# A PSUM bank per head for the logits of a two-layer DSA and MLA decoder, 64-row products in pairs, and latent transposes ahead of the reads of their bank

## The chip, the cores and the metric

The kernel runs on one core of one Trainium2 chip. The metric is the time of one execution in device microseconds; smaller is better. The engines: TensorE (PE) does matrix products, with weight loads (PEld) beside them, VectorE (DVE) and ScalarE (ACT) elementwise work, GpSimd (POOL) a few small operations, and SyncE (SP) issues most DMAs. PE writes its products into PSUM, which has eight banks; a tile of 128 partitions by 512 fp32 fills one.

## What is computed

The reference runs two post-norm layers on 256 tokens of width 2048. In each, two groups of eight heads read the same x. Group A (DSA) keeps for each query the best keys by an indexer of 16 heads of 64; group B (MLA) has queries and keys of 128 columns without and 64 with rotation, from normalised latents. A SwiGLU FFN of 5632 follows.

```python
for i in range(DEPTH):
    mix = _hybrid_mixer(x, positions, w_in[i], g_cq[i], g_ckv[i], w_uq[i], w_ukv[i], w_o[i])
    x = _layer_norm(ALPHA * x + mix, ln1_g[i], ln1_b[i])
    ffn = _swiglu(x, w_gate[i], w_up[i], w_down[i])
    x = _layer_norm(ALPHA * x + ffn, ln2_g[i], ln2_b[i])
...
q_b = jnp.einsum('bsr,re->bse', _rms_norm(cq, g_cq), w_uq).reshape(b, s, MLA_HEADS, MLA_NOPE + MLA_ROPE)
q_nope, q_pe = q_b[..., :MLA_NOPE], _rope(q_b[..., MLA_NOPE:], positions, MLA_ROPE, MLA_ROPE_THETA)
q_mla = jnp.concatenate([q_nope, q_pe], axis=-1)
k_mla = jnp.concatenate([k_nope, k_pe], axis=-1)
out_b = _causal_attention(q_mla, k_mla, v_b, (MLA_NOPE + MLA_ROPE) ** -0.5)
```

## The kernel before, in words

Weights come in units of 256 rows by 512 columns and are split into two parts (`parts`): ACT rounds the high part `wh` (L308), DVE subtracts it for the low part `wl` (L309). Each product of a projection is then three (L330 to L332: high by high, low by high, high by low). The 256 tokens are two tiles t of 128. The projections follow one another; what belongs to attention is written as tasks (generators) that `tick()` takes a step further between weight units. Behind that, a scheduler orders the instructions anew on each engine, so that the order of the code is not that of the chip; engines wait for one another by semaphores on tiles.

PSUM is shared by turns: `acc()` gives banks 0 to 3 (projections), `trp()` 4 and 5 (transposes), `att()` 6 and 7 (attention).

An attend (`attend`, two heads j) takes one bank for each token tile t. MLA's `logits` (L646) writes a 128-row product of `qn` and `kn` (L652) and adds a 64-row one of `qpT` and `kpT` (L653), head by head and tile by tile: 128 columns for t = 0, 256 for t = 1. The rows of `qpT` lie by head pairs on one half of the partitions. DVE scales and masks (L455), the softmax follows, PE transposes the weights and multiplies with the values (the PV step, L474, L475) into a bank of `att()`. The products here are fp32, unsplit. There are four MLA attends and four DSA attends per layer. The indexer (L581) multiplies 64-row operands in pairs, on both halves of the partitions, into two banks.

`tb_post` normalises the latents (`rms`) and transposes them: for each tile t, `rms_T` of k into `ckvT` (PE L350, then ACT L353 for the high and DVE L354 for the low part), `dup_T` of the rotated key into the same bank and on to `kpT` (ACT L521), and `rms_T` of q into `cqT`.

In the FFN, 10 of 11 chunks of 512 columns run through `gate_up`, which computes gate and up (`c11`, `c21`, `c12`, `c22`: the part of token tile 0 or 1 in gate or up) with Winograd's seven products p1 to p7 in place of eight for half of the rows. p2, p4 and p3 are added into c11, c21 and c12 in PSUM; DVE combines the rest at the chunk's end: L894 (e), L899 (v), L900, L905 (g, from c21), L906, L907 (v, reads c22), L911 (e, reads c12). `hidden` then multiplies (L820), and PE transposes its result (T). Every second chunk has a group of the down projection inside (`group`). `BANKS` gives each product its bank: c11 4, c21 5, c12 6, c22 7, p1 0, p5 to p7 1 to 3.

Of the kernel before, what the change touches and what calls it, by code (L numbers as in the profile page):

```python
# [31 lines left out]
P = 128  # L32
# [46 lines left out]
def hybrid_trunk(ctx: ExitStack, tc: tile.TileContext, x, xt_in, pos, w_in, g_cq, g_ckv, w_uq,  # L79
# [46 lines left out]
    def in_turn(s, first, n):  # L126
        turns[s] = turns.get(s, -1) + 1
        return bank(first + turns[s] % n, s)
# [7 lines left out]
    def att():  # L136
        return in_turn("att", 6, 2)

# [306 lines left out]
    def attend(logits_of, scale, bias, v_of, oh, ol, h0):  # L445


        lgs = []
        for t in range(NT):
            n = P * (t + 1)  # L450
            lp = att()
            for j in range(2):
                logits_of(h0 + j, t, lp[:, j * n:(j + 1) * n], n)
            lg = t2([P, 2, n], "lg")
            nc.vector.scalar_tensor_tensor(  # L455
                lg, lp[:, :2 * n].rearrange("p (j n) -> p j n", j=2), scale,
                bias[t].unsqueeze(1).to_broadcast([P, 2, n]), op0=ALU.mult, op1=ALU.add)
            for j in range(2):
                softmax_head(lg[:, j, :], t, n)
            lgs.append(lg)  # L460
        yield 3
        prs = []
        for j in range(2):
            tp = trp()
            transpose4([lgs[0][:, j, :], lgs[1][:, j, 0:P], lgs[1][:, j, P:]], tp)
            pr = t2([P, 3 * P], "pr")
            nc.scalar.activation(pr, tp[:, :3 * P], AF.Copy)
            prs.append(pr)
        yield 1
        op = att()  # L470
        for j, pr in enumerate(prs):
            v0, v1 = v_of(h0 + j)
            ov = op[:, j * S:(j + 1) * S]
            mm(ov, v0, pr[:, 0:S], start=True, stop=False)  # L474
            mm(ov[:, P:], v1, pr[:, S:], start=False, stop=True)  # L475
        split(oh.rearrange("p j t -> p (j t)"), ol.rearrange("p j t -> p (j t)"), op)


    def layer(l, xh, xl, norms, last):
# [37 lines left out]

        def dup_T(dst, t, s, tp):

            transpose4([s.rearrange("p a b -> p (a b)")], tp)  # L520
            nc.scalar.activation(dst[:, t * P:(t + 1) * P], tp[:, :P], AF.Copy)  # L521

        def ta_post(o):
            ss = []
            for t in range(NT):
                nc.vector.tensor_scalar(wi[t], o[t][:, 0:I_HEADS], IW_SCALE, None, ALU.mult)
                ss.append(dup_rope(o[t][:, 16:80], cosI[t], sinI[t], I_ROT))
                nc.scalar.activation(cq[t][:, 0:432], o[t][:, 80:512], AF.Copy)
            yield 2
            for t in range(NT):  # L530
                dup_T(kiT, t, ss[t], trp())

# [10 lines left out]

        def rms_T(y, n, dst, t, tp):
            transpose4([y[:, i * P:(i + 1) * P] for i in range(n // P)], tp)
            tv = tp[:, :n].rearrange("p (k t) -> p k t", t=P)
            split(dst[:, 0, :, t * P:(t + 1) * P], dst[:, 1, :, t * P:(t + 1) * P], tv)

        def tb_post(o):
# [12 lines left out]
            for t, (yk, yq) in enumerate(ys):  # L562
                yield 1
                tp = trp()
                rms_T(yk, KVL, ckvT, t, tp[:, P:])
                dup_T(kpT, t, sd[t], tp)
                rms_T(yq, QL, cqT, t, trp())

        def indexer():
            yield from behind(p_ta, p_qi0, p_qi1)  # L570
            score = [pt([P, P * (t + 1)], F32, f"score{t}") for t in range(NT)]
            for t in range(NT):
                n = P * (t + 1)
                per = C // n
                for h0 in range(0, I_HEADS, 2 * per):
                    rp = [att() for _ in range(2)]
                    for j in range(per):
                        for r in range(2):
                            h = h0 + 2 * j + r
                            pr = slice(64 * r, 64 * r + 64)  # L580
                            mm(rp[r][:, j * n:(j + 1) * n], qiT[h // 8][pr, h // 2 % 4, t * P:(t + 1) * P],  # L581
                               kiT[pr, :n], start=True, stop=True)
                    rl = []
                    for r in range(2):
                        s = t2([P, per, n], "rel")
                        nc.scalar.activation(s.rearrange("p j n -> p (j n)"), rp[r], AF.Relu)
                        rl.append(s)
# [52 lines left out]
        def mla_attend(hp, m, wait, *before):  # L640
# [6 lines left out]

            def logits(h, t, dst, n):
                r = h // 2 % 2
                pr = slice(64 * r, 64 * r + 64)  # L650
                ts = slice(t * P, (t + 1) * P)
                mm(dst, qn[:, h % 4, ts], kn[:, h % 4, :n], start=True, stop=False)  # L652
                mm(dst, qpT[pr, 2 * (h // 4) + h % 2, ts], kpT[pr, :n], start=False, stop=True)  # L653

# [18 lines left out]
        def dsa_attend(hp, kaT, qaT, va, wait, *before):  # L673
# [5 lines left out]

            def logits(h, t, dst, n):  # L680
                mm(dst, qaT[:, h % 4, t * P:(t + 1) * P], kaT[:, h % 4, :n], start=True, stop=True)

# [147 lines left out]

        BANKS = {"c11": 4, "c21": 5, "c12": 6, "c22": 7, "p1": 0, "p5": 1, "p6": 2, "p7": 3}
        INTO = {"p2": "c11", "p4": "c21", "p3": "c12"}

        def gate_up(fc, plain, wino, between):
# [4 lines left out]
            def passes(name, lhs, ks, w, final):  # L839
                if name not in o:  # L840
                    o[name] = bank(BANKS[name], "gu_" + name)
                for j, k in enumerate(ks):
# [204 lines left out]
```

## Time and profile before

| | |
|---|---|
| median of 3 runs | 2238.47 us (2237.68 to 2239.29) |
| the profiled execution | 2240.56 us, of which the span is 2238.5 us |
| mean granted clock of TensorE | 0.996 of full speed |
| PE busy | 2194.0 us, 98% |
| DVE busy | 1702.2 us, 76% |
| ACT busy | 1193.1 us, 53% |

The profile is of one execution. PE is busy nearly throughout, so its own timeline and the list of what it waited for are the views to start with; the busy share of another engine says little until it is taken stretch by stretch.

### The profile page before, as it was taken

How to read it: one execution, taken by the hardware profiler on the slowest of the kernel's cores; microseconds unless marked ns; L12 is line 12 of the kernel's file. 1: busy time of each engine (PE TensorE's matmuls, PEld its weight loads, DVE VectorE, ACT ScalarE, POOL GpSimd, SP SyncE). 2: the span in 40 equal slices, each digit the busy share in tenths (PEclk: the TensorE clock that was granted, in tenths of full speed). 3: DMA queues.
4: the chain of work that ended last, by engine and by line, in shares of the span. 5: the costliest groups of instructions: out<-in, count | busy, mean ns of one | idle time of the engine just before them, and what ended most of it. 6: DMA issues, size and time to landing. Idle time of an engine off the chain costs nothing. (4 is left out here: it accounts for less than half of the span.)

```text
span 2238.5 us, 27874 instructions
## 1 busy us (share of the span) xinstructions
PE 2194.0 (98%) x10128; PEld 1809.4 (81%) x10128; DVE 1702.2 (76%) x2215; ACT 1193.1 (53%) x1537; POOL 110.2 (5%) x198
## 2 busy tenths in 40 slices
PE   8999999999999999999999999999999999999997
PEld 7878788788888887887777887887888888888885
DVE  6675556987968788699667756569879697887985
ACT  5555443654555555555545554445546555555563
POOL 0100000100000000100101000001000100000002
PEclk9999999999999999999999999999999999999998
DMA  8544445656576766756655455556655757576574
GB/s 300 162 154 149 143 166 181 242 170 207 180 234 206 245 189 225 201 204 201 204 173 166 141 166 165 174 174 226 206 186 201 223 201 244 178 250 210 193 258 115
DMA packets 126057, 437.04 MB, mean 195 GB/s; under 512 B 14320, under 2 KB 14368, under 8 KB 125664
## 3 DMA queue, kind: packets, MB, share of 16 engines
q1 hardware_dynamic: 113760, 409.26, 54.0%
q0 software_dynamic: 12160, 26.01, 5.9%
q8 instruction: 79, 1.29, 0.2%
q14 instruction: 58, 0.48, 0.1%
HBM read 416.33 MB, written 2.10 MB: 187 GB/s over the span
## 5 line engine op out<-in xcount | busy, mean ns | idle before, releaser
L309 DVE TENSOR_TENSOR wl<-raw,wh 128x1024 fp32r<-128x1024 f32 (+1 forms) x892 | 1068.9, 1218 | 448.8 <-ACT wh L308 441.9
L308 ACT ACTIVATE wh<-raw 128x1024 fp32r<-128x1024 f32 (+1 forms) x892 | 926.9, 1055 | 873.9 <-PE acc L332 392.1
L846 PE MATMUL gu_c<-wh,xh 128*128 128x512 f32 x800 | 314.1, 393 | 6.7 <-DVE g L905 6.5
L848 PE MATMUL gu_c<-wl,xh 128*128 128x512 f32 x800 | 311.3, 389 | 0.0
L849 PE MATMUL gu_c<-wh,xl 128*128 128x512 f32 x800 | 311.3, 390 | 0.0
L330 PE MATMUL acc<-wh,xh 128*128 128x512 f32 (+1 forms) x768 | 303.0, 395 | 6.3 <-ACT wh L308 6.3
L331 PE MATMUL acc<-wl,xh 128*128 128x512 f32 (+1 forms) x768 | 299.1, 389 | 3.6 <-DVE wl L309 3.6
L332 PE MATMUL acc<-wh,xl 128*128 128x512 f32 (+1 forms) x768 | 297.9, 388 | 0.0
L330 PE MATMUL acc<-wh,hT 128*128 128x512 f32 x640 | 249.0, 389 | 0.9 <-DVE v L906 0.9
L331 PE MATMUL acc<-wl,hT 128*128 128x512 f32 x640 | 249.1, 389 | 0.5 <-DVE wl L309 0.5
L332 PE MATMUL acc<-wh,hT 128*128 128x512 f32 x640 | 248.8, 389 | 0.0
L871 DVE TENSOR_TENSOR raw<-raw,raw 128x1024 f32<-128x1024 f32 x160 | 195.5, 1223 | 8.4 <-DMA raw<-in_w_up_dram 5.0
L846 PEld LDWEIGHTS gu_c<-wh,xh 128*128 128x128 f32 x800 | 150.2, 188 | 41.0 <-DVE g L905 10.2
L849 PEld LDWEIGHTS gu_c<-wh,xl 128*128 128x128 f32 x800 | 150.2, 188 | 31.5
L330 PEld LDWEIGHTS acc<-wh,xh 128*128 128x128 f32 x768 | 144.7, 189 | 37.9 <-ACT wh L308 7.1
L848 PEld LDWEIGHTS gu_c<-wl,xh 128*128 128x128 f32 x800 | 150.2, 188 | 30.5 <-DVE wl L309 0.3
L331 PEld LDWEIGHTS acc<-wl,xh 128*128 128x128 f32 x768 | 145.3, 189 | 32.0 <-DVE wl L309 6.1
L332 PEld LDWEIGHTS acc<-wh,xl 128*128 128x128 f32 x768 | 145.0, 189 | 27.9
L330 PEld LDWEIGHTS acc<-wh,hT 128*128 128x128 f32 x640 | 120.1, 188 | 26.2 <-DVE v L906 1.3
L331 PEld LDWEIGHTS acc<-wl,hT 128*128 128x128 f32 x640 | 120.1, 188 | 25.7 <-DVE wl L309 0.9
L332 PEld LDWEIGHTS acc<-wh,hT 128*128 128x128 f32 x640 | 120.1, 188 | 24.9
L941 POOL DMA_DIRECT2D x<-d x64 | 55.0, 875 | 1135.4 <-ACT d L940 1108.5
(235 smaller groups left out, 2611.3 us busy)
## 6 DMA issues: line engine op xcount, KB each, us to landing
raw<-in_w_gate_dram SPq DMA_DIRECT2D x176, 512.0 KB, 4.7
raw<-in_w_up_dram SPq DMA_DIRECT2D x176, 512.0 KB, 4.7
raw<-in_w_down_dram SPq DMA_DIRECT2D x176, 512.0 KB, 5.1
raw<-in_w_in_dram SPq DMA_DIRECT2D x144, 512.0 KB, 3.4
raw<-in_w_o_dram SPq DMA_DIRECT2D x64, 512.0 KB, 3.3
x<-d POOLq DMA_DIRECT2D x64, 256.0 KB, 6.4
raw<-in_w_in_dram SPq DMA_DIRECT2D x16, 400.0 KB, 3.0
raw<-in_w_uq_dram SPq DMA_DIRECT2D x12, 512.0 KB, 3.3
```

The lines of the kernel that those rows point to most:

```text
L308: nc.scalar.activation(wh[:, :n], raw[:, :n], AF.Copy)
L309: nc.vector.tensor_tensor(wl[:, :n], raw[:, :n], f(wh[:, :n]), op=ALU.subtract)
L330: mm(o[t][:, :n], h, a, start=first, stop=False)
L331: mm(o[t][:, :n], h, b, start=False, stop=False)
L332: mm(o[t][:, :n], l, a, start=False, stop=final)
L846: mm(o[name], h, a, start=name not in begun, stop=False)
L848: mm(o[name], h, b, start=False, stop=False)
L849: mm(o[name], l, a, start=False, stop=end)
L871: nc.vector.tensor_tensor(d, x, y, op=ADD)
L941: nc.gpsimd.dma_start(sl, d, accum_op=ALU.add)
```

## The change

`att()` gives one tile over both banks 6 and 7. An attend takes one such tile, with a bank for each head in place of one for each token tile: the four 128-row products of MLA go first, then the 64-row ones in pairs, head 0 on partitions 0 to 63, head 1 on 64 to 127 (the host's permutation of the columns goes). Both token tiles' masks read that tile. The PV result takes a bank of `trp()`. The indexer's two banks come as one tile too, and so do c12 and c22 of `gate_up`. In `tb_post` all three transposes of a token tile come ahead of the reads of their banks.

```diff
     def att():
-        return in_turn("att", 6, 2)
+        return ps.tile([P, 2, C], F32, name=nm("att"), tag="b67", bufs=1)
...
+        lp = att()
+        logits_of(h0, [[lp[:, j, 0:P], lp[:, j, P:3 * P]] for j in range(2)])
         for t in range(NT):
             n = P * (t + 1)
-            lp = att()
-            for j in range(2):
-                logits_of(h0 + j, t, lp[:, j * n:(j + 1) * n], n)
             lg = t2([P, 2, n], "lg")
...
-        op = att()
+        op = trp()
...
-                tp = trp()
-                rms_T(yk, KVL, ckvT, t, tp[:, P:])
-                dup_T(kpT, t, sd[t], tp)
-                rms_T(yq, QL, cqT, t, trp())
+                tp, tq = trp(), trp()
+                rms_T(yk, KVL, tp[:, P:])
+                dup_T(sd[t], tp)
+                rms_T(yq, QL, tq)
+                rms_out(KVL, ckvT, t, tp[:, P:])
+                dup_out(kpT, t, tp)
+                rms_out(QL, cqT, t, tq)
...
-            def logits(h, t, dst, n):
-                r = h // 2 % 2
-                pr = slice(64 * r, 64 * r + 64)
-                ts = slice(t * P, (t + 1) * P)
-                mm(dst, qn[:, h % 4, ts], kn[:, h % 4, :n], start=True, stop=False)
-                mm(dst, qpT[pr, 2 * (h // 4) + h % 2, ts], kpT[pr, :n], start=False, stop=True)
+            def logits(h0, dst):
+                ts = [slice(t * P, (t + 1) * P) for t in range(NT)]
+                for j in range(2):
+                    for t in range(NT):
+                        h = (h0 + j) % 4
+                        mm(dst[j][t], qn[:, h, ts[t]], kn[:, h, :P * (t + 1)], start=t == 0, stop=False)
+                for t in range(NT):
+                    for j in range(2):
+                        pr = slice(64 * j, 64 * j + 64)
+                        mm(dst[j][t], qpT[pr, h0 // 2, ts[t]], kpT[pr, :P * (t + 1)], start=False, stop=t == NT - 1)
...
-        BANKS = {"c11": 4, "c21": 5, "c12": 6, "c22": 7, "p1": 0, "p5": 1, "p6": 2, "p7": 3}
+        BANKS = {"c11": 4, "c21": 5, "p1": 0, "p5": 1, "p6": 2, "p7": 3}
...
                 if name not in o:
-                    o[name] = bank(BANKS[name], "gu_" + name)
+                    if name in BANKS:
+                        o[name] = bank(BANKS[name], "gu_" + name)
+                    else:
+                        pair = att()
+                        o["c12"], o["c22"] = pair[:, 0, :], pair[:, 1, :]
```

What this does to the order of the instructions is seen at three places. First, PE at the latents of layer 0: `dup` is the rotated key, `rn` a normalised latent, `qiT` the indexer's queries, `acc` a projection. Before, from the dup transpose of tile 0 to the transposes of tile 1:

```order
L330 MATMUL acc_1039<-wh_1156,xh_67 128x512
L350 MATMUL tr_1140<-ident,dup_981 128x128 [waits DVE_49]
L331 MATMUL acc_1039<-wl_1157,xh_67 128x512
L332 MATMUL acc_1039<-wh_1156,xl_69 128x512
L581 MATMUL att_1172<-kiT_393,qiT_82 128x256 [waits Activation_49]
L581 MATMUL att_1173<-kiT_393,qiT_82 128x256 [waits Activation_49]
L581 MATMUL att_1172<-kiT_393,qiT_82 128x256
L581 MATMUL att_1173<-kiT_393,qiT_82 128x256
L350 MATMUL tr_1186<-ident,rn_1019 128x128 [waits Activation_49]
L350 MATMUL tr_1186<-ident,rn_1019 128x128
L350 MATMUL tr_1193<-ident,rn_1027 128x128 [waits DVE_49]
L350 MATMUL tr_1193<-ident,rn_1027 128x128 x3
```

After, the transposes of tile 0, and then what stands ahead of those of tile 1:

```order
L333 MATMUL acc_1036<-wh_1119,xl_69 128x512
L351 MATMUL tr_1135<-ident,rn_1000 128x128 [waits DVE_49]
L351 MATMUL tr_1135<-ident,rn_1000 128x128
L351 MATMUL tr_1135<-ident,dup_978 128x128
L351 MATMUL tr_1136<-ident,rn_1008 128x128 [waits DVE_49]
L351 MATMUL tr_1136<-ident,rn_1008 128x128 x3
```

```order
L332 MATMUL acc_1036<-wl_1152,xh_67 128x512
L333 MATMUL acc_1036<-wh_1151,xl_69 128x512
L589 MATMUL att_1167<-kiT_393,qiT_82 128x256 [waits PE_49,Activation_49]
L589 MATMUL att_1167<-kiT_393,qiT_82 128x256 x3
L351 MATMUL tr_1180<-ident,rn_1016 128x128 [waits Activation_49]
L351 MATMUL tr_1180<-ident,rn_1016 128x128
L351 MATMUL tr_1180<-ident,dup_990 128x128
L351 MATMUL tr_1181<-ident,rn_1024 128x128 [waits DVE_49]
```

The dup transpose of tile 0 has moved from the middle of a projection unit, where it waited for DVE, to the other transposes of its tile; those of tile 1 wait for ACT, which copies to kpT.

Second, PE at the end of an FFN chunk of layer 0 (`gu_c21`, `gu_c12`, `gu_c11` and the tile `att` are c21, c12, c11, and c12 with c22, with running numbers behind; p3 is the product with `s`). Before, p3 stands behind c21's last products (p4), and the next chunk's c11 follows:

```order
L846 MATMUL gu_c211080_5067<-wh1145_5372,xh779_3632 128x512
L848 MATMUL gu_c211080_5067<-wl1146_5373,xh779_3632 128x512
L849 MATMUL gu_c211080_5067<-wh1145_5372,xl780_3633 128x512
L846 MATMUL gu_c121087_5098<-wh1148_5386,s4827_3861 128x512 [waits Activation_49]
L848 MATMUL gu_c121087_5098<-wl1149_5387,s4827_3861 128x512 [waits DVE_49]
L849 MATMUL gu_c121087_5098<-wh1148_5386,s4828_3862 128x512
L846 MATMUL gu_c121087_5098<-wh1148_5386,s4827_3861 128x512
L848 MATMUL gu_c121087_5098<-wl1149_5387,s4827_3861 128x512
L849 MATMUL gu_c121087_5098<-wh1148_5386,s4828_3862 128x512
L846 MATMUL gu_c111156_5410<-wh1154_5406,xh763_3513 128x512 [waits DVE_49,Activation_49]
L848 MATMUL gu_c111156_5410<-wl1155_5407,xh763_3513 128x512 [waits DVE_49]
```

After, p4 is followed by 24 products of the next chunk (c11, then c21), of which the last two are seen here, then p3:

```order
L870 MATMUL gu_c211140_5400<-wl1143_5410,xh765_3618 128x512
L871 MATMUL gu_c211140_5400<-wh1142_5409,xl766_3619 128x512
L868 MATMUL att1071_5082<-wh1131_5369,s4813_3847 128x512 [waits DVE_49]
L870 MATMUL att1071_5082<-wl1132_5370,s4813_3847 128x512
L871 MATMUL att1071_5082<-wh1131_5369,s4814_3848 128x512
L868 MATMUL att1071_5082<-wh1131_5369,s4813_3847 128x512
L870 MATMUL att1071_5082<-wl1132_5370,s4813_3847 128x512
L871 MATMUL att1071_5082<-wh1131_5369,s4814_3848 128x512
L351 MATMUL tr1149_5451<-ident_70,silu1135_5384 128x128 [waits DVE_49]
L351 MATMUL tr1149_5451<-ident_70,silu1135_5384 128x128 x3
L868 MATMUL att1147_5431<-wh1145_5427,xh749_3499 128x512 [waits DVE_49,Activation_49]
```

p3 has moved behind 24 products of the next chunk, and its first product waits for DVE alone.

Third, DVE at the same chunk end. Before, from L900 to the product with the up part:

```order
L900 TENSOR_TENSOR e1134_5320<-e1134_5320,gu_p51105_5178 128x512 [waits DVE_49]
L905 TENSOR_TENSOR g11147_5382<-gu_c211080_5067,v71144_5368 128x512 [waits PE_49]
L911 TENSOR_TENSOR e1134_5320<-e1134_5320,gu_c121087_5098 128x512 [waits DVE_49,PE_49]
L906 TENSOR_TENSOR v71144_5368<-v71144_5368,gu_p51105_5178 128x512 [waits DVE_49]
L820 TENSOR_TENSOR silu1151_5398<-silu1151_5398,e1134_5320 128x512 [waits DVE_49,Activation_49]
L907 TENSOR_TENSOR v71144_5368<-v71144_5368,gu_c221088_5105 128x512 [waits DVE_49]
L309 TENSOR_TENSOR wl1175_5499<-raw1173_5496,wh1174_5498 128x1024 [waits DMAHW0_49]
L820 TENSOR_TENSOR silu1152_5401<-silu1152_5401,v71144_5368 128x512 [waits DVE_49,Activation_49]
```

After, from L922 (L900 before), with g at L927 (L905), v at L928 and L929 (L906, L907), and e at L933 (L911):

```order
L922 TENSOR_TENSOR e1117_5303<-e1117_5303,gu_p51088_5161 128x512 [waits DVE_49]
L927 TENSOR_TENSOR g11130_5365<-gu_c211064_5051,v71127_5351 128x512 [waits PE_49]
L310 TENSOR_TENSOR wl1152_5461<-raw1150_5458,wh1151_5460 128x1024 [waits DMAHW7_49,Activation_49]
L928 TENSOR_TENSOR v71127_5351<-v71127_5351,gu_p51088_5161 128x512 [waits DVE_49]
L310 TENSOR_TENSOR wl1157_5481<-raw1155_5478,wh1156_5480 128x1024 [waits DMAHW0_49,Activation_49]
L929 TENSOR_TENSOR v71127_5351<-v71127_5351,att1071_5082 128x512 [waits DVE_49]
L310 TENSOR_TENSOR wl1160_5499<-raw1158_5496,wh1159_5498 128x1024 [waits DMAHW1_49,Activation_49]
L838 TENSOR_TENSOR silu1135_5384<-silu1135_5384,v71127_5351 128x512 [waits DVE_49,Activation_49]
L933 TENSOR_TENSOR e1117_5303<-e1117_5303,att1071_5082 128x512 [waits PE_49]
L310 TENSOR_TENSOR wl1163_5517<-raw1161_5514,wh1162_5516 128x1024 [waits DMAHW2_49,Activation_49]
L838 TENSOR_TENSOR silu1134_5381<-silu1134_5381,e1117_5303 128x512 [waits DVE_49]
```

Weight splits now stand between the additions, and the one that reads c12 has moved behind the one that reads c22 and the first product.

## Rows read from the trace of the kernel before

**Rows 1.** It is the page's part 1: busy time, share of the span and instructions of each engine, PE first.

```profile
PE 2194.0 (98%) x10128; PEld 1809.4 (81%) x10128; DVE 1702.2 (76%) x2215; ACT 1193.1 (53%) x1537; POOL 110.2 (5%) x198
```

**Rows 2.** The waits of PE in the whole span, grouped by what was waited for; columns: us in total, times, longest.

```profile
PE gu_c L846 <- DVE g L905: 6.5, 6, 1.7
PE tr L350 <- DVE ckvT L354: 6.4, 3, 3.1
PE acc L330 <- ACT wh L308: 6.3, 2, 5.9
```

**Rows 3.** PE's timeline over the first MLA attend, the start of the second and the last one; columns: start, duration, instruction, and in brackets idle time before it. An x2 row is the two passes of one fp32 product; the duration runs over both and past the next start.

```profile
151.12 0.39 PE L652 MATMUL att<-kn,qn 128*128 128x128 f32 x2
151.44 0.48 PE L653 MATMUL att<-kpT,qpT 64*128 64x128 f32 x2
...
152.68 0.70 PE L652 MATMUL att<-kn,qn 128*128 128x256 f32 x2
153.31 0.70 PE L653 MATMUL att<-kpT,qpT 64*128 64x256 f32 x2
...
155.19 0.50 PE L330 MATMUL acc<-wh,xh 128*128 128x512 f32 x1
155.53 0.39 PE L331 MATMUL acc<-wl,xh 128*128 128x512 f32 x1
...
164.13 0.39 PE L652 MATMUL att<-kn,qn 128*128 128x128 f32 x2
...
1372.74 0.39 PE L652 MATMUL att<-kn,qn 128*128 128x128 f32 x2
...
1376.82 0.50 PE L330 MATMUL acc<-wh,xh 128*128 128x512 f32 x1
```

**Rows 4.** PE's timeline over the start of the PV step of the first MLA attend (L474, L475: 256 and 128 columns, all with 128 contraction rows), same columns.

```profile
171.08 0.60 PE L474 MATMUL att<-pr,vb 128*128 128x256 f32 x2
171.51 0.38 PE L475 MATMUL att<-pr,vb 128*128 128x128 f32 x2
171.73 0.60 PE L474 MATMUL att<-pr,vb 128*128 128x256 f32 x2
```

**Rows 5.** PE's timeline over one step of the indexer (L581: four products of 64 rows and 256 columns, in pairs on the two halves of the rows and in two banks) and the projection's products behind it, same columns.

```profile
106.94 1.14 PE L581 MATMUL att<-kiT,qiT 64*128 64x256 f32 x8
108.00 0.50 PE L330 MATMUL acc<-wh,xh 128*128 128x512 f32 x1
108.34 0.40 PE L331 MATMUL acc<-wl,xh 128*128 128x512 f32 x1
```

**Rows 6.** Busy time of each engine in two stretches, with their number of instructions; the first is one FFN chunk from p7 to p7, the second the next chunk, which has a down group in it. Behind the engines: granted clock, DMA share, GB/s.

```profile
571.12:612.85 41.73, 41.73 (x189) 34.62 (x188) 40.26 (x42) 23.98 (x27) 0.00 (x0) 1.00 0.50 172
612.85:655.00 42.15, 41.70 (x188) 34.32 (x187) 28.94 (x30) 22.90 (x26) 3.50 (x4) 1.00 0.83 273
```

**Rows 7.** PE's timeline at the transposes of the latents, layer 0 and layer 1.

```profile
113.58 0.39 PE L330 MATMUL acc<-wh,xh 128*128 128x512 f32 x1
117.10 0.47 PE L350 MATMUL tr<-ident,dup 128*128 128x128 f32 x1 [3.13 <-DVE ckvT L354]
...
1228.42 0.33 PE L350 MATMUL tr<-ident,dup 128*128 128x128 f32 x1 [3.11 <-DVE ckvT L354]
```

**Rows 8.** The timeline of DVE and ScalarE (ACT) around the first of these.

```profile
115.49 1.22 DVE L309 TENSOR_TENSOR wl<-raw,wh 128x1024 fp32r<-128x1024 f32 x1
116.63 0.42 DVE L354 TENSOR_TENSOR ckvT<-tr,ckvT 128x256 fp32r<-128x256 f32 x1
...
117.61 0.28 ACT L521 ACTIVATE kpT<-tr 128x128 f32<-128x128 f32 x1 [4.73 <-PE tr L350]
```

**Rows 9.** Busy time and granted clock (the column behind POOL) in the stretches behind the two long latent waits, and in one of the FFN with a wait in it.

```profile
117.00:121.00 4.00, 3.90 (x18) 2.43 (x18) 1.87 (x3) 1.87 (x4) 0.00 (x0) 0.58 0.39 131
1228.50:1233.00 4.50, 4.50 (x20) 3.25 (x21) 2.93 (x6) 3.29 (x6) 0.00 (x0) 0.63 0.49 138
872.00:880.00 8.00, 6.30 (x29) 4.87 (x28) 7.24 (x11) 5.63 (x7) 0.00 (x0) 1.00 0.65 244
```

**Rows 10.** The timeline of PE and DVE at the end of a chunk at which DVE lags: p7's start, the subtraction g, and the first product that waits for it.

```profile
867.75 0.39 PE L846 MATMUL gu_p<-wh,s 128*128 128x512 f32 x1
...
874.56 0.68 DVE L905 TENSOR_TENSOR g<-gu_c,v 128x512 f32<-128x512 f32 x1
...
875.30 0.50 PE L846 MATMUL gu_c<-wh,xh 128*128 128x512 f32 x1 [1.70 <-DVE g L905]
```

**Rows 11.** The timeline of PE and DVE at the end of a chunk at which DVE runs on time: p7's start, and DVE's operations behind it.

```profile
571.13 0.39 PE L846 MATMUL gu_p<-wh,s 128*128 128x512 f32 x1
...
572.16 1.22 DVE L309 TENSOR_TENSOR wl<-raw,wh 128x1024 fp32r<-128x1024 f32 x1
...
573.29 0.68 DVE L899 TENSOR_TENSOR v<-e,gu_p 128x512 f32<-128x512 f32 x1
...
575.62 0.68 DVE L905 TENSOR_TENSOR g<-gu_c,v 128x512 f32<-128x512 f32 x1
...
576.22 0.68 DVE L911 TENSOR_TENSOR e<-e,gu_c 128x512 f32<-128x512 f32 x1
```

**Rows 12.** The timeline of DVE and PE behind the PV step of the first MLA attend: DVE's split of its result, and the next attend's transposes.

```profile
173.51 0.68 DVE L354 TENSOR_TENSOR oB<-att,oB 128x512 fp32r<-128x512 f32 x1
...
177.85 0.38 PE L350 MATMUL tr<-ident,lg 128*128 128x128 f32 x2
```

More of the change, by code (lines that the diff above doesn't have):

```diff
@@ L448, in attend @@
         lgs = []
+        lp = att()
+        logits_of(h0, [[lp[:, j, 0:P], lp[:, j, P:3 * P]] for j in range(2)])
         for t in range(NT):
             n = P * (t + 1)
-            lp = att()
-            for j in range(2):
-                logits_of(h0 + j, t, lp[:, j * n:(j + 1) * n], n)
             lg = t2([P, 2, n], "lg")
-            nc.vector.scalar_tensor_tensor(
-                lg, lp[:, :2 * n].rearrange("p (j n) -> p j n", j=2), scale,
-                bias[t].unsqueeze(1).to_broadcast([P, 2, n]), op0=ALU.mult, op1=ALU.add)
+            nc.vector.scalar_tensor_tensor(lg, lp[:, :, t * P:t * P + n], scale,
+                                           bias[t].unsqueeze(1).to_broadcast([P, 2, n]), op0=ALU.mult, op1=ALU.add)
             for j in range(2):
@@ L516, in dup_rope, with dup_T, dup_out @@
             return s
-        def dup_T(dst, t, s, tp):
+        def dup_T(s, tp):
             transpose4([s.rearrange("p a b -> p (a b)")], tp)
+        def dup_out(dst, t, tp):
             nc.scalar.activation(dst[:, t * P:(t + 1) * P], tp[:, :P], AF.Copy)
@@ L530, in ta_post @@
             for t in range(NT):
-                dup_T(kiT, t, ss[t], trp())
+                tp = trp()
+                dup_T(ss[t], tp)
+                dup_out(kiT, t, tp)
         def rms(src, n, g):
@@ L542, in rms, with rms_T, rms_out @@
             return y
-        def rms_T(y, n, dst, t, tp):
+        def rms_T(y, n, tp):
             transpose4([y[:, i * P:(i + 1) * P] for i in range(n // P)], tp)
+        def rms_out(n, dst, t, tp):
             tv = tp[:, :n].rearrange("p (k t) -> p k t", t=P)
@@ L575, in indexer @@
                 for h0 in range(0, I_HEADS, 2 * per):
-                    rp = [att() for _ in range(2)]
+                    rp = att()
                     for j in range(per):
@@ L580, in indexer @@
                             pr = slice(64 * r, 64 * r + 64)
-                            mm(rp[r][:, j * n:(j + 1) * n], qiT[h // 8][pr, h // 2 % 4, t * P:(t + 1) * P],
+                            mm(rp[:, r, j * n:(j + 1) * n], qiT[h // 8][pr, h // 2 % 4, t * P:(t + 1) * P],
                                kiT[pr, :n], start=True, stop=True)
@@ L585, in indexer @@
                         s = t2([P, per, n], "rel")
-                        nc.scalar.activation(s.rearrange("p j n -> p (j n)"), rp[r], AF.Relu)
+                        nc.scalar.activation(s.rearrange("p j n -> p (j n)"), rp[:, r, :], AF.Relu)
                         rl.append(s)
@@ L678, in dsa_attend, with logits @@
                 oT["A"] = [t8([P, A_HEADS, S], F32R, "oA") for _ in range(2)]
-            def logits(h, t, dst, n):
-                mm(dst, qaT[:, h % 4, t * P:(t + 1) * P], kaT[:, h % 4, :n], start=True, stop=True)
+            def logits(h0, dst):
+                for j in range(2):
+                    for t in range(NT):
+                        h = (h0 + j) % 4
+                        mm(dst[j][t], qaT[:, h, t * P:(t + 1) * P], kaT[:, h, :P * (t + 1)], start=t == 0,
+                           stop=t == NT - 1)
             h0 = 2 * hp
@@ L1027 @@
     q = np.arange(M_HEADS * (M_NOPE + M_ROPE)).reshape(M_HEADS, -1)
-    pe = q[[0, 2, 1, 3, 4, 6, 5, 7], M_NOPE:]
+    pe = q[:, M_NOPE:]
     args.append([given(f"w_uq{i}", _blocks(a["w_uq"], c.reshape(-1)))
```

## The prediction

> **What bounds the kernel now.** I read the page's busy times first. TensorE (PE) is busy 2194.0 of 2238.5 us [rows 1], so it is the bound almost everywhere, and this change takes no product away: time can come only from PE's few idle stretches, or from stretches in which it counts as busy and advances slowly. The waits of PE, grouped by what they wait for, come second [rows 2]: 6.5 us for a DVE subtraction at the ends of FFN chunks (L905), 6.4 us for a DVE subtraction on the latents (L354), and 6.3 us at the start, which the change leaves alone. For slow busy time I read PE's timeline around the MLA logits [rows 3], and compared it with the same products in other company [rows 4, 5]. VectorE (DVE) is second: over one chunk it is busy 40.26 of 41.73 us while PE is busy for all of it [rows 6], so there DVE's order decides when PSUM banks come free.
>
> **The logits: -14.9 us.** In an MLA attend eight products alternate between 128 contraction rows (L652) and 64 (L653). From the first product to the next projection's second one is 155.53 - 151.12 = 4.41 us, of which that projection's first product takes one spacing of 0.23: 4.18 us net [rows 3]. The last attend agrees: 1376.82 - 1372.74 = 4.08 against 155.19 - 151.12 = 4.07. The same widths without alternation cost 0.43 (256 columns) and 0.22 (128) in the PV step [rows 4]; I use 0.213 for the second, half of the first. Four of each make 2.57, so eight changes of shape cost 1.61, or 0.20 each. After the change there are two changes of shape, 0.40. The four 128-row products stay at 2 x (0.43 + 0.213) = 1.29. What two 64-row products on the two halves cost, the indexer shows: four of 256 columns into two banks take 108.34 - 106.94 - 0.23 = 1.17 us with both edges [rows 5], where one after another they would take 1.72 and the edges; so they overlap, and each pair costs about one of its products, 0.43 + 0.21 = 0.64. The sum is 1.29 + 0.64 + 0.40 = 2.33, a gain of 1.86 per attend, 14.9 for the eight. Bounds: with no overlap the pairs cost 1.29, and the gain is 6 x 0.20 = 1.2 each, 9.8 in all; if the edges cost nothing beyond 0.1 each, 16.6.
>
> **The latent transposes: -6.9 us.** Here the wait is PE's on the subtraction into ckvT: the transpose of dup writes the bank that this subtraction reads. PE has run out of work at 113.97 and stands until 117.10 (3.13 us) in layer 0, and 3.11 us at 1228.42 in layer 1; the third wait is 0.17 [rows 2, 7]. DVE was never idle meanwhile: the subtraction starts at 116.63, straight behind a weight split, and ends at 117.05 [rows 8]. After each long wait the granted clock is lower, 0.58 over 4 us and 0.63 over 4.5, between the levels 2.4 and 1.2 GHz [rows 9]: 4 x 0.42 + 4.5 x 0.37 = 3.35 us more. Together 6.4 + 3.35 = 9.75 us. The change puts dup's transpose ahead of the reads, so this wait goes, but a smaller one comes: the transposes of the second token tile take the same bank, which the copy to kpT, queued behind the same subtraction, must have read. Without the wait PE gets there after two products (0.45), the dup transpose (0.1) and an indexer step (1.2), at 113.81 + 1.75 = 115.6. The subtraction may come some 0.3 us earlier than now, ends near 116.75, and the copy takes 0.28 [rows 8]: 117.05. That leaves 1.45 us per layer, 2.9 in all. A stall of 1.70 us elsewhere left the clock at 1.00 [rows 9, 10], so I count no slow clock: 9.75 - 2.9 = 6.9. Bounds: 0.3 (the stall comes back at the second tile with the slow clock), and 9.75.
>
> **The FFN: +9.9 us.** What the change's words don't name is that c12 and c22 of gate_up now lie in one tile. The last product of a chunk, p3, writes c12; the DVE addition that reads c22 (L907) comes ahead of it in the program, and with one tile p3 waits for it, at all twenty chunk ends. The order of after bears it out: p3's six products no longer stand behind p4, but behind 24 products of the next chunk, and DVE's additions have weight splits between them (the third piece of order above). The DVE rows give the prices: a split or an addition of two raw tiles 1.135 from start to start, a 512-column addition 0.60 [rows 11]. From the start of g (L905) to the end of the c22 addition the new order takes 0.60 + 1.135 + 0.60 + 1.135 + 0.68 = 4.15 us. There are three waits, all of PE:
> (a) c21 of the next chunk, for g. It used to stand behind p3 and up to ten products; now 5.46 us (24 products at 0.2275) after p7's start. Where DVE runs on time, g ends 575.62 + 0.60 - 571.13 = 5.1 us after it: no wait [rows 11]. Where DVE lags, as at 867.75, g ends at 875.22, 7.47 after, and PE waits 2.0 us instead of 1.70 [rows 10]. Worked out so for the nine ends with a lag, the total is 10.5 us in place of 6.5: +4.0.
> (b) p3, for the c22 addition. After c21 come 12 products (2.73 us); the addition ends 4.15 - 0.60 = 3.55 after g. That is 0.8 where nothing else stands between, and at the ends with four or five filler products nothing: five ends of layer 0 together, +2.8.
> (c) The next c12, for the addition that reads p3's result (L911), behind a split and a product on DVE: 0.4 to 0.5 us at the five ends where two products or fewer follow p3, +2.2.
> Together 9.0. Where fillers hide (b), DVE waits about 0.25 us for p3 instead, at eight ends; half of this may reach PE, +0.9. I take 9.9. Bounds: 0 (the queued products absorb everything but what PE waits now) and 14, if every one of the twenty ends pays (b) and half pay (c).
> The Trainium skill, "PSUM — Partial Sum Buffer" (PSUM bank collisions raise a hardware error), says that two engines must not use one bank and quadrant at once, and that different banks run clean. By that rule p3 and the read of c22 needn't wait for one another, and the cost would be 0, so that the sum would be -21.8. The waits in the order of after follow the tile, not the bank; no run shows it yet.
>
> **At nothing.** The PV result now takes a transpose bank. DVE's split of it starts at 173.51 and is done at 174.19, and the next transposes into these banks come at 177.85 [rows 12]: 3.7 us of cover, and the ends of the other attends look alike. One attention tile for all: the attends stand over 10 us apart [rows 3], and its readers are done about 1 us after the last product. The subtractions and maxima of the first tile's softmax start 0.4 us later, behind which the projection products run on. DSA's logits are the same four products in another order. In these cases the cost, if the cover is gone, is under 0.5 us per attend, 4 us for eight.
>
> **Sum.** -14.9 - 6.9 + 9.9 = -11.9 us. The profiled execution spans 2238.5 us (2240.56 with what lies around it), the median of the runs is 2238.47, so the difference goes to the median: 2226.5 us.
>
> **The rivals.**
> A, the forecast: 2226.5, and by the bounds taken together (about ±3 for the logits, ±4 for the latents, ±5 for the FFN, independent: ±7) 2219 to 2234. Chance 0.56.
> B, the FFN costs nothing: the 24 products and fillers that the order puts ahead cover DVE, and the lag doesn't grow. Then -21.8 + 0, 2216.7. For it: the order was made with these waits in it, and five of ten ends in layer 1 have fillers. Against it: DVE has 1.5 us of slack in a chunk of 41.7 [rows 6], and PE waits there already [rows 2]. Chance 0.16.
> C, the latent stall moves to the second tile in full, with the clock behind it: the gain of 6.9 shrinks to 0.3, 2233.1. For it: DVE's queue is the same and only the place of waiting changes; a stall of 1.45 us is an estimate, and 3.1 brought the slow clock. Against it: PE has 1.8 us of other work ahead of it. Chance 0.16.
> D, the pairs don't run at once, so that the change doesn't do what it says, and only the changes of shape are saved: 9.8 in place of 14.9, 2231.6. Against it: [rows 5]. The Trainium skill, "TensorEngine Tiling (Array Packing)" (Key Properties), says that different row tiles run independently and that only a change of tiling mode drains the array; by that rule D is out, and the trace agrees with 1.17 us for four products of 0.43. For it: these pairs add onto sums that the 128-row products have begun in the same banks, which the indexer's don't. Chance 0.07.
> E, slower: the coupling at chunk ends carries itself on. p3 is held, so the addition behind it (L911) is late, DVE stands, the splits of the next chunk are late, and with 1.5 us of slack in a chunk [rows 6] the next end starts with a larger lag. It turns the sum when each of the twenty ends costs PE 21.8 / 20 = 1.1 us; a wait of 1.70, as the longest now [rows 10], at every end gives 34 - 21.8 = +12, 2250.7. Against it: every second chunk has a down group, in which DVE is busy less (28.94 of 42.15 us) and catches up [rows 6]. Chance 0.05.
>
> **How the numbers follow.** The likeliest is A: 2226.5. The range must reach B below (0.16) and C and D above: 2216 to 2235 leaves out E, and the tails of the others, about 2 in 10. A measurement of this kernel can tell about 0.2% (4.5 us) from no change, so faster means under 2234.0 and slower over 2243.0. A is faster in nearly all of its range (0.53 of 0.56), B always (0.16), D mostly (0.05 of 0.07), C in a bit over half (0.09 of 0.16): faster 0.83. E is slower 0.04 of 0.05; the rest, 0.13, is the same.
>
> **What would show it.** The attends: first logit to next projection 2.3 us net in place of 4.18, the two products of a pair starting nearly together; 3.1 would be D. The latents: one wait of about 1.5 us per layer ahead of the second tile's transposes, and a granted clock of 1.00 behind it; 3 us and a clock near 0.6 would be C. The FFN: waits of PE for g (L905) near 10 us, and new ones for the c22 addition and the one behind p3 of 5 us in all; none of these would be B, over 25 us E. The forecast is wrong above all if DVE's lag at the chunk ends comes out otherwise than in the trace of before, since every FFN number hangs on it.

## The result

The changed kernel takes 2224.76 us (median, 2223.74 to 2225.12) against 2238.88 us for the kernel before beside it: ratio 0.9936, 95% interval 0.9918 to 0.9953. The forecast was 2226.5, faster. The profiled execution took 2223.74 us, its span is 2221.9 us against 2238.5.

Part 1 of the page of after, as [rows 1]:

```profile
PE 2179.9 (98%) x10128; PEld 1800.6 (81%) x10128; DVE 1699.9 (77%) x2215; ACT 1191.0 (54%) x1537; POOL 109.0 (5%) x198
```

PE has the same 10128 records and is busy 14.1 us less: it does the same products in less busy time. Where, the timeline of the first MLA attend of after shows, as [rows 3] (x8 is eight passes, four fp32 products):

```profile
146.28 1.48 PE L663 MATMUL att<-kn,qn 128*128 128x128 f32 x8
147.69 0.93 PE L667 MATMUL att<-kpT,qpT 64*128 64x128 f32 x8
148.54 0.50 PE L331 MATMUL acc<-wh,xh 128*128 128x512 f32 x1
148.88 0.39 PE L332 MATMUL acc<-wl,xh 128*128 128x512 f32 x1
```

From the first logit to the second projection product it is 148.88 - 146.28 = 2.60 us, in place of 4.41; less one spacing 2.37. The two pairs take 148.54 - 147.69 = 0.85 to the next product, where the prediction had 0.64 and one change of shape (0.20).

PE's waits of after, as [rows 2]:

```profile
PE acc L331 <- ACT wh L309: 6.8, 3, 6.1
PE gu_c L868 <- DVE g L927: 6.2, 6, 1.5
...
PE att L868 <- DVE v L929: 1.7, 4, 0.5
PE gu_c L868 <- ACT wh L309: 1.6, 1, 1.6
...
PE tr L351 <- ACT kpT L522: 1.4, 2, 1.0
PE acc L331 <- DVE v L928: 0.3, 1, 0.3
PE att L868 <- DVE e L933: 0.3, 1, 0.3
```

The wait for ckvT (6.4 us) is gone, and the one for the kpT copy ahead of the second tile has come, 1.4 us in place of the 2.9 forecast. New are the waits for v (L929), at p3, and for e (L933), at the c12 behind it. The stretches behind the kpT waits, as [rows 9], have the full clock (column behind POOL):

```profile
115.90:120.00 4.10, 4.08 (x22) 3.49 (x23) 3.30 (x7) 3.22 (x7) 0.00 (x0) 1.00 0.62 177
1222.50:1227.00 4.50, 4.32 (x23) 3.72 (x24) 3.71 (x7) 3.63 (x8) 0.00 (x0) 1.00 0.57 186
```

One chunk end of layer 0 of after, PE and DVE, the view that [rows 10, 11] show of before:

```profile
608.81 0.68 DVE L927 TENSOR_TENSOR g<-gu_c,v 128x512 f32<-128x512 f32 x1
...
609.55 0.50 PE L868 MATMUL gu_c<-wh,xh 128*128 128x512 f32 x1 [1.50 <-DVE g L927]
...
610.54 0.68 DVE L928 TENSOR_TENSOR v<-v,gu_p 128x512 f32<-128x512 f32 x1
...
612.28 0.68 DVE L929 TENSOR_TENSOR v<-v,att 128x512 f32<-128x512 f32 x1
...
613.01 0.50 PE L868 MATMUL att<-wh,s 128*128 128x512 f32 x1 [0.45 <-DVE v L929]
```

PE waits for g (c21), then runs twelve products, then p3 waits until v has read c22, though p3 writes the other bank. From g's start to the end of the c22 addition it is 612.28 + 0.68 - 608.81 = 4.15 us, exactly the price of the prediction.

To see where the 16.5 us of the span went, the same instruction is looked for in both traces (the first transpose of the latents, the first logit of each attend, the first p1 of the first chunk with Winograd's products, the first transpose behind the FFN) and the change of its distance to the one before is taken. These are differences of start times in the two timelines, in us:

| stage | forecast | after | after, second execution | before, second execution |
|---|---|---|---|---|
| latents, layer 0 | -6.9 for both | -4.14 | -4.18 | -0.02 |
| latents, layer 1 | | -4.55 | -4.55 | +0.30 |
| logits, eight attends | -14.9 | -14.50 | -14.50 | -0.03 |
| FFN, layer 0 | +9.9 for both | +7.45 | +6.66 | +1.51 |
| FFN, layer 1 | | -0.06 | +0.30 | -1.79 |

The last two columns are two of the runs below: the attention repeats within 0.3 us, the FFN of one layer only within 2.

Three of the marks in layer 0 (the first transpose of the latents, the first p1, the first transpose behind the FFN), before:

```profile
110.86 0.82 PE L350 MATMUL tr<-ident,rn 128*128 128x128 f32 x6
...
459.87 0.39 PE L846 MATMUL gu_p<-wh,xh 128*128 128x512 f32 x1
...
1110.32 0.86 PE L350 MATMUL tr<-ident,x 128*128 128x128 f32 x6 [0.57 <-DVE x L377]
```

And after:

```profile
110.16 0.38 PE L351 MATMUL tr<-ident,rn 128*128 128x128 f32 x2
...
447.80 0.39 PE L868 MATMUL gu_p<-wh,xh 128*128 128x512 f32 x1
...
1105.70 1.07 PE L351 MATMUL tr<-ident,x 128*128 128x128 f32 x8 [0.56 <-DVE x L378]
```

The FFN of layer 0 takes 1110.32 - 459.87 = 650.45 us before and 657.90 after. The stages sum to -15.8 us; the other 0.7 lies ahead of the first mark, where the twelve other traces differ from that of before by -0.7 to +0.7 us, whatever the kernel.

### The profile page after: what moved, and what is told of

Read it like the earlier page. It is cut to its first block, busy times and chain, and to the rows that moved or that the text cites. A ratio compares the mean times of both kernels' runs of the same rounds, so it can differ in the third digit from the quotient of the medians.

```text
span 2221.9 us, 27847 instructions
## 1 busy us (share of the span) xinstructions
PE 2179.9 (98%) x10128; PEld 1800.6 (81%) x10128; DVE 1699.9 (77%) x2215; ACT 1191.0 (54%) x1537; POOL 109.0 (5%) x198
## 5 line engine op out<-in xcount | busy, mean ns | idle before, releaser
L868 PE MATMUL gu_c<-wh,xh 128*128 128x512 f32 x480 | 187.6, 391 | 7.8 <-DVE g L927 6.2
L870 PE MATMUL gu_c<-wl,xh 128*128 128x512 f32 x480 | 187.2, 390 | 0.0
L871 PE MATMUL gu_c<-wh,xl 128*128 128x512 f32 x480 | 186.9, 389 | 0.0
L868 PE MATMUL att<-wh,xh 128*128 128x512 f32 x320 | 127.7, 399 | 0.4 <-DVE e L933 0.3
L871 PE MATMUL att<-wh,xl 128*128 128x512 f32 x320 | 125.0, 391 | 0.0
L870 PE MATMUL att<-wl,xh 128*128 128x512 f32 x320 | 125.0, 391 | 0.0
L868 PEld LDWEIGHTS gu_c<-wh,xh 128*128 128x128 f32 x480 | 90.0, 188 | 29.7 <-DVE g L927 9.0
```

What stands on the lines that cost most here:

```text
L868: mm(o[name], h, a, start=name not in begun, stop=False)
L870: mm(o[name], h, b, start=False, stop=False)
L871: mm(o[name], l, a, start=False, stop=end)
```

## The experiments

**Theory.** The gain is -14.5 us from the logits (fewer changes of shape, and pairs that overlap) and -8.7 from the latents; the loss of 7.4 comes from c12 and c22 in one tile, by the wait of p3. **Rivals:** the loss is DVE's lag, which an earlier start moves; the logits owe part of their gain to the bank per head; the latents' gain is another edit's.

**1. A tile for each bank.**

```diff
-        return ps.tile([P, 2, C], F32, name=nm("att"), tag="b67", bufs=1)
+        return [bank(6 + j, "att") for j in range(2)]
...
-            nc.vector.scalar_tensor_tensor(lg, lp[:, :, t * P:t * P + n], scale,
-                                           bias[t].unsqueeze(1).to_broadcast([P, 2, n]), op0=ALU.mult, op1=ALU.add)
+            for j in range(2):
+                nc.vector.scalar_tensor_tensor(lg[:, j, :], lp[j][:, t * P:t * P + n], scale, bias[t],
+                                               op0=ALU.mult, op1=ALU.add)
...
-                        o["c12"], o["c22"] = pair[:, 0, :], pair[:, 1, :]
+                        o["c12"], o["c22"] = pair
```

(The indexer's two banks are two tiles again as well.)

> The changed kernel, but banks 6 and 7 are two tiles again, so that c12 and c22 of gate_up no longer share one; each head's logits then take their own DVE operation for scale and mask (16 more small ones per layer half). Theory: the FFN's 7.4 us (the trace of the changed kernel loses 7.4 us in layer 0 between the first and the last FFN chunk and nothing in layer 1, against before) come from the shared tile, so this kernel takes 7 us less than the changed one, about 2217.5, and all of it in layer 0's FFN; the attends stay at 2.4 us. Rival: the loss comes from DVE being later after the faster attention (another lag at the chunk ends), then the time stays near 2224.8. Second rival: the separate mask operations cost DVE so much at the attends that the gain there shrinks; then the 16 attends (DSA's too) show it, by at most 0.5 us each, 2222 to 2225.

Measured: 2219.01 us, ratio 0.9901 (0.9887 to 0.9914), against 0.9936 for the changed kernel: 7.8 us of 2240 less. In the trace the FFN of layer 0 is 0.36 us shorter than before (not 7.45 longer), the logits are -14.52, and the list of PE's waits has no line for v or e:

```profile
PE gu_c L869 <- DVE g L928: 7.5, 8, 2.1
...
PE tr L351 <- ACT kpT L523: 3.6, 2, 1.8
```

The scheduler put p3 behind p4 again. The loss is the shared tile's.

**2. The tile kept, c22 read early.**

```diff
                 p("p6", slhs("s2"), r11, lo_)
                 if final:
+                    q = t2([P, C], "q22")
+                    nc.scalar.activation(q, o["c22"], AF.Copy)
+                    nc.vector.tensor_tensor(q, q, o["p5"], op=ADD)
...
-                    nc.vector.tensor_tensor(v, v, o["p5"], op=ADD)
-                    nc.vector.tensor_tensor(v, v, o["c22"], op=ADD)
+                    nc.vector.tensor_tensor(v, v, q, op=ADD)
```

> The changed kernel with the shared tile kept, but c22 is read early: ACT copies it to SBUF behind p6, DVE adds p5 to the copy there, and at the chunk's end only that sum is added to v. So p3 has no DVE read of its tile to wait for, and one DVE operation moves from the end of the chunk to its middle. Theory: the loss is the wait of p3 for the c22 addition and what the scheduler does around it, so the order goes back to p3 behind p4 and the time to 2217.5 or a little less (one 0.6 us operation fewer ahead of g and e at twenty ends: up to 4.5 us of waits for g shrink), 2213 to 2218. Rival: DVE is the limit over a chunk, not p3's wait; the same number of DVE operations then gives the same time, near 2224.8, or more, since ACT has 20 copies of 0.6 us more.

Measured: 2216.61 us, ratio 0.9891 (0.9878 to 0.9905). FFN -0.05 in layer 0 and -0.88 in layer 1. PE's waits of this kernel:

```profile
PE gu_c L868 <- DVE g L930: 6.4, 8, 1.3
PE acc L331 <- ACT wh L309: 6.1, 1, 6.1
PE acc L332 <- DVE wl L310: 3.9, 4, 1.2
PE tr L351 <- ACT v L396: 3.4, 3, 1.1
PE tr L351 <- ACT kpT L522: 2.0, 2, 1.0
PE tr L351 <- DVE x L378: 1.5, 3, 0.6
PE gu_p L870 <- DVE wl L310: 0.6, 1, 0.6
```

This is the whole list. With the same tile and no read in p3's way the wait is gone, and p3 stands behind p4. So it is not the tile by itself, but the read that p3 has to let by. The edit also takes one addition off DVE at the chunk's end; run 3 shows what that is worth.

**3. The early read on the kernel before, and on separate tiles.** The same edit on two other kernels.

> The kernel before with c22 read early and nothing of the change. Theory: with a tile of its own for c22 nothing is held, so the early read can only take one 0.6 us operation from DVE's way between p7 and the end of a chunk: the waits for g (6.5 us in all) shrink a little, 2236 to 2238 by the first trace's scale, between -0.1% and none. Rival: the early read is worth 7 us by itself, whatever the tiles: 2231.

> The kernel with two tiles for banks 6 and 7 and c22 read early. Theory: both edits remove the same wait, so together they give no more than either: 2216 to 2219 on the scale of 2240.8 for the kernel before. Rival: they add up, 2212 to 2214.

Measured: 2236.98 us, 0.9988 (0.9980 to 0.9996), on the kernel before; with separate tiles 2217.40 us, 0.9896 (0.9881 to 0.9911). The early read gives 0.1% by itself, in the trace by shorter waits for g (4.0 us in place of 6.5, or of 5.2 in the second execution of before). With separate tiles it gives nothing that differs from run 1 or run 2. The two edits remove one wait.

**4. The latents alone, and the change without them.** The `tb_post` part of the diff alone on the kernel before, and all but that part.

> The kernel before with the latent transposes ahead of their reads, and nothing else of the change. Theory: the two latent places give 4.15 and 4.55 us, as they do in the trace of the changed kernel, 8.7 in all: 2230.2. Rival: some of the 8.7 is owed to the indexer's single tile (its products come sooner) or is given back later, where DVE is then the later engine: 2232 to 2235. Granted clock near 1.00 behind both places by the theory.

> The changed kernel with the latent transposes as before: the dup transpose behind the read of its bank. By the trace of the changed kernel the latents are worth 4.15 and 4.55 us, so +8.7, 2233.5. By the latents alone on the kernel before (3.35 and 1.4 us in the trace, the second with a granted clock of 0.74 to 0.84 behind the wait) they are worth 4.7: 2229.5. What tells them apart is whether the waits for the kpT copy are short (1.0 and 0.35 us) because of the other edits, or by how an execution falls.

Measured: alone 2236.19 us, 0.9980 (0.9969 to 0.9990), some 4.6 us; the rest of the change without it 2231.34 us, 0.9955 (0.9941 to 0.9968), which is 4.3 us (0.0019) short of the changed kernel, though these two intervals overlap. Both are half of 8.7. The stages are the surer reading: alone -3.35 in layer 0 and -1.42 in layer 1; the change without them -1.00 and -2.35. So of -4.14 and -4.55 the transposes account for 3.1 and 2.2, and the rest came with the other edits: the dup transpose waits 2.34 us in layer 0 without the transposes' part, in place of 3.13, so the subtraction comes sooner. My theory was wrong in that point. The order of the logits has no part in it: with that of before (run 6) the stages are -4.16 and -4.56. The one tile for both banks has: with separate tiles (run 1) the kpT waits are 1.8 us each and the gains -3.34 and -3.06, the first of them that of the latents alone. Whether it is the indexer's tile or the one mask operation, no run here isolates.

In layer 1 of the latents alone a part of the gain went to the clock. PE's timeline, and two stretches (granted clock behind POOL):

```profile
1229.44 0.51 PE L350 MATMUL tr<-ident,rn 128*128 128x128 f32 x2 [1.82 <-ACT kpT L523]
...
1230.67 0.78 PE L330 MATMUL acc<-wh,xh 128*128 128x512 f32 x1
1231.24 0.63 PE L331 MATMUL acc<-wl,xh 128*128 128x512 f32 x1
```

```profile
1227.00:1231.00 4.00, 2.18 (x14) 1.75 (x12) 3.31 (x7) 1.89 (x4) 0.00 (x0) 0.84 0.55 203
1231.00:1235.00 4.00, 4.00 (x15) 3.17 (x14) 3.90 (x10) 1.51 (x5) 0.00 (x0) 0.74 0.45 165
```

The first two projection products behind the wait start 0.57 us apart. In run 1 the same wait left the clock alone, and they start 0.31 us apart:

```profile
1218.28 0.44 PE L351 MATMUL tr<-ident,rn 128*128 128x128 f32 x2 [1.81 <-ACT kpT L523]
...
1219.02 0.47 PE L331 MATMUL acc<-wh,xh 128*128 128x512 f32 x1
1219.33 0.39 PE L332 MATMUL acc<-wl,xh 128*128 128x512 f32 x1
```

```profile
1218.00:1222.00 4.00, 3.72 (x20) 3.21 (x21) 3.31 (x6) 3.19 (x7) 0.00 (x0) 1.00 0.52 166
```

**5. Both products of a pair on one half.**

```diff
-                        pr = slice(64 * j, 64 * j + 64)
-                        mm(dst[j][t], qpT[pr, h0 // 2, ts[t]], kpT[pr, :P * (t + 1)], start=False, stop=t == NT - 1)
+                        h = h0 + j
+                        pr = slice(64 * (h // 2 % 2), 64 * (h // 2 % 2) + 64)
+                        mm(dst[j][t], qpT[pr, 2 * (h // 4) + h % 2, ts[t]], kpT[pr, :P * (t + 1)],
+                           start=False, stop=t == NT - 1)
...
```

(The host's order of the columns is that of before.)

> The changed kernel, but the two 64-row products of a pair lie on the same half of the partitions (the host's permutation of before is kept), so that they can't run beside each other; the number of changes of shape is the same. Theory: overlap is worth one product of each pair, 0.43 + 0.21 = 0.64 us per attend, eight attends: +5.1, 2229.9, attends of 3.05 us net in place of 2.4. Rival: the gain is all from the changes of shape, and the pairs overlap no more than neighbours on one half do: no difference, 2224.8.

Measured: 2231.97 us, 0.9957 (0.9943 to 0.9970). The first attend of this kernel:

```profile
147.68 1.47 PE L663 MATMUL att<-kn,qn 128*128 128x128 f32 x8
149.08 1.57 PE L668 MATMUL att<-kpT,qpT 64*128 64x128 f32 x8
150.59 0.50 PE L331 MATMUL acc<-wh,xh 128*128 128x512 f32 x1
150.92 0.39 PE L332 MATMUL acc<-wl,xh 128*128 128x512 f32 x1
```

The same four 64-row products take 150.59 - 149.08 = 1.51 us in place of 0.85: 0.66 for the overlap, against 0.64 forecast. The eight attends sum to -9.31, so 5.2 of the 14.5 are overlap and 9.3 the six changes of shape less in each attend, 0.19 for each change.

**6. The order of before in the new banks.** The 64-row product of a head and tile directly behind its 128-row one, on the new halves.

> The changed kernel with its banks and halves, but the logits in the order of before: for each token tile and head the 128-row product and at once the 64-row one. Theory: eight changes of shape at 0.2 us and no overlap make 4.2 us net per attend in place of 2.4, eight attends +14.5: 2239. Rival: the bank per head or the one mask operation per tile have a part in the gain; then attends of 3 to 3.8 us, 2230 to 2236.

Measured: 2240.86 us, 0.9998 (0.9989 to 1.0007). The eight attends differ from before by 0.00 us in sum. Banks, halves and the one mask operation give nothing without the new order. With the logits' gain gone, the latents' gain and the FFN's loss cancel.

**7. Each kernel once more.**

> The kernel before, unchanged, profiled a second time and on another chip, so that the stages of two traces of one kernel can be set side by side. The latents alone lost 3.1 us again between the first and the last FFN chunk of layer 0, whose code they don't touch. If that is how far the lag of DVE at the chunk ends differs from one execution to the next, this trace differs from the first one by up to 3 us there and by under 0.3 us in the attention stages. If it is a consequence of the earlier start, this trace agrees with the first within 0.5 us everywhere.

> The changed kernel unchanged, beside the two above on one chip. Theory: the FFN of layer 0 again takes 6.5 to 8.5 us longer than in the kernel before and that of layer 1 within 1.5 us of it, as in the three other kernels with the shared tile (7.4, 8.0 and 9.2 us in layer 0); 0.9936 of the time of the kernel before, within 0.002. Rival: the layers differ by how an execution falls, and layer 1 shows some of it this time.

Measured: before 2240.88 us, 0.9997 (0.9987 to 1.0006); changed 2223.95 us, 0.9930 (0.9918 to 0.9942). The stages are in the table above. The FFN's loss is layer 0's again (+6.66, in the other three kernels with the shared tile and the late read, runs 5, 6 and 4, +7.95, +9.22 and +7.32; of the +9.22 some 1.7 is a stretch at a low clock, shown in the last section), with -0.06 to +2.0 in layer 1. That the latents alone lost 3.1 us in the FFN of layer 0 is partly how executions differ (1.5 here); the rest stays open.

**8. The kpT copy first.** Run 2 with the copy of dup ahead of the two reads of the latent.

> The kernel with c22 read early, and the copy of dup to kpT put ahead of the two reads of the latent, so that the transposes of the second token tile wait for the DVE subtraction itself and no longer for a copy behind it. Theory: the wait of 1.0 us in each layer shrinks by the copy's 0.28 us and its hand-over, 0.35 each, and stays below what brings the slow clock: -0.7, 2216 on the scale of 2216.6. Rival: the subtraction, one queue place behind on ACT, is later by the same 0.3: no difference.

Measured: 2216.71 us, 0.9893 (0.9879 to 0.9906): no difference from run 2. The wait is then for the subtraction itself, 1.4 us in two in place of 2.0, but the stages of the latents agree with run 2 within 0.1. A copy less behind the subtraction is not worth what was expected.

The version of run 2, 1.1% faster than the kernel before, beats both kernels. It shows that the change as written leaves 0.45% of the time (0.9936 to 0.9891) at the chunk ends: by run 1 the shared tile's wait is 0.35% of it, and by run 3 the early read is worth 0.1% by itself.

## Why the prediction came out as it did

**The logits** were right in size and mechanism: -14.5 against -14.9, with the two parts at 5.2 and 9.3 against 5.1 and 9.8 (runs 5, 6). The rows of the indexer and of the PV step gave the prices of products that the old trace did not contain. Rival D is out.

**The latents** were right in mechanism, short in size: -8.7 against -6.9. The wait that takes the old one's place was counted at 1.45 us per layer and is 1.0 and 0.35. The step that failed is "the subtraction may come some 0.3 us earlier than now": it ends at 115.56, 1.5 us earlier than 117.05, of which 0.7 is the earlier start of the whole stretch; and by run 4 some of that is owed to the other edits. In the changed kernel:

```profile
115.14 0.42 DVE L355 TENSOR_TENSOR ckvT<-tr,ckvT 128x256 fp32r<-128x256 f32 x1
...
115.92 0.44 PE L351 MATMUL tr<-ident,rn 128*128 128x128 f32 x2 [1.01 <-ACT kpT L522]
```

"I count no slow clock" held for the changed kernel; in the latents alone rival C's wait with a lower clock behind it came in one of the two layers, with 1.8 us in place of 3. So C did not happen here, but the reason given against the slow clock, one stall of 1.70 us without it, was too weak (last section).

**The FFN** was right in sign and cause (runs 1, 2), and mis-sized: +7.4 against +9.9. Its terms, as the time from one of PE's starts to the next beyond the usual one, in the two traces:

- (b) p3's wait for v: 0.5 to 0.6 at each of four ends of layer 0, 2.3 against 2.8 forecast; none in layer 1, as its fillers promised.
- (c) the wait of the c12 behind it, for e: 0.44, 0.37, 0.12 and 0.13 at the same four ends, 1.1 in place of 2.2. Four other ends of layer 0 have 0.12 to 0.13 each, 0.5, where the prediction added 0.9 for DVE's own waits for p3; DVE did wait for it 13 times, 3.7 us in all.
- (a) failed. The waits for g were to grow from 6.5 to 10.5; they are 6.2 in the list. In layer 0 they grew from 3.3 to 3.9 so counted, in layer 1 they shrank from 4.1 to 3.3. The lags of DVE in the old trace were taken over end by end, though the new order changes them; the prediction named this as its weakest point.

In its place came a wait that I had not listed: PE for a weight's high part (ACT wh) at two ends of layer 0, 1.77 + 0.57. At the first of them ACT had itself waited, by the trace for DVE's e (L922), before it took that unit. These terms make 6.8 us in layer 0; two waits for a weight's low part in the trace of before, 1.0 in all, are gone; the remaining 1.6 of the 7.45 lies in spacings too short to be listed as waits, and was not traced to a cause. The sum is closer than its terms: that 2.3 us came from a wait not listed, where (a) was to bring 4.0, is luck.

**At nothing** held: the PV result in a transpose bank and the late mask of the first tile show no wait of PE, and from the start of one attend to that of the next the time changes by -1.81 us behind MLA's and by under 0.1 us behind DSA's. **Rival B** is what the kernel could have had, and runs 1 and 2 have it. Its reason, that the fillers would cover DVE, held in layer 1 alone. **Rival E** did not happen: the lag does not carry itself on.

The rule of the Trainium skill that was set beside the FFN ("PSUM — Partial Sum Buffer", PSUM bank collisions raise a hardware error), that accesses to different banks run clean, is borne out as far as these runs go: with the two banks as two tiles (run 1) the same p3 comes ahead of the read of c22, and the FFN of layer 0 loses nothing (-0.36 us). At one end of that run, PE starts a product into the next c12 at 1972.91, while DVE reads c22 from 1972.38 to 1973.06. It is the bookkeeping by tile that waits.

## What to carry to other kernels

A gain in an attention step can be given back in a quite different one that shares its PSUM tags: after such an edit look at who else takes the tile, and whether a read in program order stands ahead of a write to the tile's other bank. If so, move the read early or give the banks tiles of their own. Products of different contraction heights were cheapest here sorted by height, since each change of shape cost 0.2 us, and then paired on the two halves. Stalls that end in a DVE queue are not properties of an instruction: price them with a range, as the queue ahead of them moves with every other edit.

## What was not expected of the hardware

Waits of PE of the same length were followed by different clocks. In the latents alone (run 4) the wait of 1.82 us in layer 1 was followed by a granted clock of 0.74, a mean between the levels 2.4 and 1.2 GHz. The wait of 1.81 us in the same place of layer 0 of the same kernel left it at 1.00, as the one of run 1 did:

```profile
117.46 0.44 PE L350 MATMUL tr<-ident,rn 128*128 128x128 f32 x2 [1.81 <-ACT kpT L523]
...
118.00:122.00 4.00, 4.00 (x22) 3.35 (x20) 3.57 (x7) 3.14 (x7) 0.00 (x0) 1.00 0.61 231
```

At a chunk end of run 6 a wait of 1.51 us was followed by 3.5 us at 0.51, which cost 3.5 x 0.49 = 1.7 us, while the waits of 1.50 us at 609.55 in the changed kernel and of 1.70 us before [rows 9, 10] were followed by 1.00:

```profile
617.34 0.50 PE L866 MATMUL gu_c<-wh,xh 128*128 128x512 f32 x1 [1.51 <-DVE g L925]
...
617.70:621.20 3.50, 3.50 (x10) 2.76 (x9) 3.50 (x5) 2.67 (x4) 0.00 (x0) 0.51 0.92 325
```

In layer 0 of the change without the transposes' part (run 4) a wait of 2.34 us was followed by 0.58:

```profile
115.70:119.70 4.00, 4.00 (x18) 2.53 (x18) 1.76 (x2) 1.96 (x4) 0.00 (x0) 0.58 0.39 131
```

The length of a wait thus does not tell by itself whether the clock falls behind it, and what decides is not shown by these runs.
